# An encoder layer with expert retrieval on one core: Gelu of a score block emitted one block later, transposes of the picks later, gather share 0.68

## The chip, the cores and the metric

The kernel runs on one core of one Trainium2 chip. Its time is the device time of one launch in microseconds; the kernel before has a median of 1366.46 us over three runs (1363.83 to 1366.56). Five engines work side by side, each through its own queue in order: PE multiplies matrices, DVE and ACT work on elements, POOL issues the gathers and does small element work, SP issues the loads of weights and tables. An instruction at the head of a queue that waits for a semaphore holds back all that stand behind it.

## The reference

Two sequences (prompt and sample, 256 tokens each, width 1024) go through the same layer: a gated convolution and an attention with 16 meta tokens, both projected out and added to the input, and then an expert retrieval, which is where this case plays:

```
s = einsum('thpc,hpnc->thpn', q, subkeys)          # 8 heads, 2 halves, 128 keys each
sv, si = top_k(s, 16)                              # of each half
cv, cp = top_k(sv[0][:,None] + sv[1][None], 16)    # 16 pairs of a head: 128 experts a token
eidx  = si[0]*128 + si[1]  of these pairs;  gates = softmax(cv)
a   = gelu(einsum('thkd,td->thk', u_tab[eidx], x), approximate=False) * gates
out = einsum('thk,thkd->td', a, v_tab[eidx])
```

There are 16384 experts (128 times 128), each with a row of 1024 in `u_tab` and in `v_tab`.

## The kernel before, in words

The two sequences are computed in two ways. For the prompt's 256 tokens the picked rows are **gathered**: one gather fetches, for one pick k of a tile of 128 tokens, each token's row of u and v side by side (128 x 2048 f32, 1.05 MB, line 157). DVE multiplies the u half with the token and sums it (the dot, `grow<-grow,xg`), ACT takes Gelu and multiplies the gate (two instructions on `dots`), and DVE adds v times that weight to the token's accumulator (the value, `hg<-grow,dots,hg`). Two tiles times 128 picks make 256 such gathers. Four buffers hold them (`GBUF`), so gather n+4 is issued once value n has been added. When value 128 is done, the accumulator of tile 0 is written out (line 166, `out_yp<-hg`) and that of tile 1 is loaded into the same buffer (line 168, `hg<-hdram`); value 129 waits for both.

The sample's 256 tokens are computed **dense**, over all experts, in two stages that PE runs:

- The *score stage* (lines 913 to 928) has 128 blocks. Block j loads 512 KB of u (line 918), multiplies it with the tokens (8 fp32 matmuls `pSj<-xr,u`; the profile lists each as two rows) into one of four PSUM buffers of the pool `psS`, and ACT takes Gelu of it. Block j+4 needs that buffer again.
- The *value stage* (lines 939 to 953) has 128 blocks, each with 512 KB of v and matmuls `acc<-v,Al` or `acc<-v,Ah` into four accumulators.

Beside the score blocks a generator, `gates_dense`, works off the dense gates: it decodes the sample's picks into `idx_i` and `idx_j` (`fin1`, DVE work), transposes them on PE (lines 864 to 867, `pi` and `pg`), and then in 32 steps for each of two tiles builds one-hot rows on DVE and ACT (`oi`, `oj`, `gh`, `gl`), multiplies them on PE into a 128 x 128 table of gates for four tokens (8 fp16 matmuls `pgm`, a *gate group* below), and puts that into `Al` or `Ah`. Where a block's Gelu stands already, the group is multiplied onto it (columns below `r_done`); where not, the block's Gelu is multiplied by the gates that stand (`n = tau[0]` tokens have theirs): ACT writes Gelu of those to `pSj` itself and DVE forms the product (`Al<-pSj,Al`).

The order of the work is set by credits and then by a scheduler. After each score block `bg(3.5)` gives the generator 3.5 times `SBS` and the gathers 3.5 times `SS`; a step of the generator costs what it yields, a step of the gathers costs `GU` = 2.65. A step of the gathers emits the weight of one pick, the dot of the next, and the issue of a further gather; that issue also waits for the matmuls of the block last emitted (`pe_mark`). The scheduler of the tile framework then orders each engine's instructions. The value stage spreads the gathers that are left evenly: `want = left * (j + 1) // (P - 2)`.

Of the kernel before, what the change touches and what calls it, by code (L numbers as in the profile page):

```python
# [12 lines left out]
AF = mybir.ActivationFunctionType  # L13
ALU = mybir.AluOpType
# [22 lines left out]
SF = 0.5  # L37
SB0 = 0.35
SR = 0.6
SS = 0.64  # L40
SMAX = 0.7
SBS = 0.42

# [2 lines left out]
def encoder_layer(ctx: ExitStack, tc: tile.TileContext, xp, xs_, meta, vec, w_in, w_out, wq,  # L46
# [22 lines left out]
    dve = Recorded(nc.vector, last)  # L69
    act = Recorded(nc.scalar, last_act)  # L70

    def sb(name, bufs, side="left"):
        return tc.tile_pool(name=name, bufs=bufs, side=side, reuse_waits="tile")
# [32 lines left out]
    def wtile(name):  # L106
        return wp.tile([P, D], F32, tag="w", name=name)
# [16 lines left out]
    def mm(out, st_, mv, chunks=range(NC), split=False):  # L124

        terms = ((0, 0), (0, 1), (1, 0)) if split else ((0, 0),)
        n = 0
        for c in chunks:
            for a, b in terms:
                i = pe.matmul(out, st_(c, a), mv(c, b), start=(n == 0), stop=(n == NC * len(terms) - 1))  # L130
                n += 1
        pe_mark[0] = i
        return i
# [80 lines left out]
    def run_tasks(limit=None):  # L214
        while tasks and (limit is None or credit["b"] >= 0):
            try:
                credit["b"] -= next(tasks[0])
            except StopIteration:
                tasks.pop(0)

    def bg(us):
        if tasks:
            credit["b"] += us * share["b"]
            run_tasks(1)
        credit["a"] += us * (share["a"] if tasks else min(share["a"] + share["b"], SMAX))
        more(0.0)

    def more(us):
        credit["a"] += us
        while credit["a"] >= GU:  # L230
            credit["a"] -= GU
            gather()
# [558 lines left out]
    def A(j):  # L791
        return Al[:, j] if j < JH else Ah[:, j - JH]
# [52 lines left out]
    r_done = [0]  # L845
    tau = [0]

    def gates_dense():

        for t in range(2):  # L850
            yield from fin1(t)
        q1x.close()
        topk_left[0] = -1
        ogx = ExitStack()
        og = ogx.enter_context(sb("og", 1, "right"))
        io = og.tile([P, P], F16, name="io")
        act.dma_start(io, iota16)
        ident16 = og.tile([P, P], F16, name="ident16")
        dve.tensor_copy(ident16, ident)
        iv = io.rearrange("p (a r) -> p a r", r=2)  # L860
        v4 = lambda x: x.rearrange("p t (a r) -> p t a r", r=2)
        for t in range(2):
            pi = psg.tile([P, 2, P], F16, tag="g", name="pi")
            pe.transpose(pi[:, 0, :], idx_i[:, t], ident16)
            pe.transpose(pi[:, 1, :], idx_j[:, t], ident16)
            pg = psg.tile([P, P], F32, tag="g", name="pg")
            pe.transpose(pg, gate_all[:, 2 + t], ident)
            glo = og.tile([P, P], F32, tag="glo", name="glo")
            g16 = og.tile([P, OC, P], F16, tag="gl", name="g16", bufs=2)[:, 0, :]
            dup = og.tile([P, 3, P, 2], F16, tag="dup", name="dup")  # L870
            act.activation(g16, pg, AF.Copy, scale=GSH)
            dve.scalar_tensor_tensor(glo, pg, GSH, g16, op0=ALU.mult, op1=ALU.subtract)
            for r in range(2):
                act.activation(dup[:, 0:2, :, r], pi, AF.Copy)
                act.activation(dup[:, 2, :, r], g16, AF.Copy)
            yield 1.6
            for o in range(P // OC):
                s0 = o * OC
                oi = og.tile([P, OC, P], F16, tag="oi", name="oi", bufs=2)
                oj = og.tile([P, OC, P], F16, tag="oj", name="oj", bufs=2)  # L880
                gh = og.tile([P, OC, P], F16, tag="gh", name="gh", bufs=2)
                gl = og.tile([P, OC, P], F16, tag="gl", name="gl", bufs=2)
                sl4 = lambda k: dup[:, k, s0:s0 + OC, None, :].to_broadcast([P, OC, 64, 2])
                ib = iv[:, None, :, :].to_broadcast([P, OC, 64, 2])
                dve.tensor_tensor(v4(oi), sl4(0), ib, op=ALU.is_equal)
                dve.tensor_tensor(v4(oj), sl4(1), ib, op=ALU.is_equal)
                dve.tensor_tensor(v4(gh), v4(oj), sl4(2), op=ALU.mult)
                for q in range(OC):
                    act.activation(gl[:, q, :], oj[:, q, :], AF.Copy, scale=glo[:, s0 + q:s0 + q + 1])
                for q in range(OC // 4):  # L890
                    pg = psg.tile([P, 4, P], F32, tag="g", name="pgm")
                    for r in range(4):
                        k = 4 * q + r
                        pe.matmul(pg[:, r, :], oi[:, k, :], gh[:, k, :], start=True, stop=False)  # L894
                        pe.matmul(pg[:, r, :], oi[:, k, :], gl[:, k, :], start=False, stop=True)
                    a = t * P + s0 + 4 * q
                    n = r_done[0]
                    pj = pg.rearrange("p t j -> p j t")
                    for part, lo, hi in ((Al, 0, JH), (Ah, JH, P)):
                        m = min(max(n, lo), hi)  # L900
                        if m > lo:
                            av = part[:, 0:m - lo, a:a + 4]
                            dve.scalar_tensor_tensor(av, pj[:, lo:m], 1.0 / GSH, av, op0=ALU.mult, op1=ALU.mult)
                        if m < hi:
                            act.activation(part[:, m - lo:hi - lo, a:a + 4], pj[:, m:hi], AF.Copy, scale=1.0 / GSH)
                tau[0] = t * P + s0 + OC
                yield 1.3 + (4 * r_done[0] + 60) / 700
        ogx.close()

    tasks.append(gates_dense())  # L910
    share.update(a=SS, b=SBS)
    ut = {}
    for j in range(P):
        if j == 80:
            while topk_left[0] >= 0:
                next(tasks[0], None) is None and tasks.pop(0)
        ub = wtile("u")
        nc.sync.dma_start(ub, u_t[:, j])
        p = psS.tile([P, 256], F32, tag="S", name="pSj")
        mm(p, lambda c, k: ub[:, c * P:(c + 1) * P], xr1)  # L920
        n = tau[0]
        if n:
            act.activation(p[:, :n], p[:, :n], AF.Gelu)
            dve.tensor_tensor(A(j)[:, :n], p[:, :n], A(j)[:, :n], op=ALU.mult)
        if n < 256:
            act.activation(A(j)[:, n:], p[:, n:], AF.Gelu)
        r_done[0] = j + 1
        bg(3.5)
    run_tasks()

    vp = ctx.enter_context(sb("vp", 2, "right"))
# [97 lines left out]
```

## Time and profile before

| what | us or as named |
|---|---|
| median of three runs | 1366.46 |
| time of the profiled execution | 1362.99 |
| its span, first to last instruction | 1360.9 |
| busy PE, DVE, ACT, POOL | 1298.1, 1031.9, 437.4, 414.0 |
| first matmul of the score stage | 401.23 |
| first matmul of the value stage | 907.5 |
| end of the last matmul | 1357.1 |
| mean DMA rate over the span | 338 GB/s |

A row of a group of instructions reads: line, engine, operation, tile written and tiles read, count, busy time and mean duration, and the idle time of the engine just before with what ended it. A row of the timeline reads: start, duration, engine, line, operation, tiles, shapes, count, and in brackets the idle time before it. Line 63 is a helper through which all DVE and ACT instructions go, so these are told apart by their tiles. The ends of matmuls are modelled; their starts, and the distance between starts, are measured.

### The profile page before, as it was taken

What the parts mean: (1) busy time and instruction counts of PE and PEld (TensorE: products, weight loads), DVE (VectorE), ACT (ScalarE), POOL (GpSimd) and SP (SyncE); (2) the same over time, 40 slices, a digit from 0 to 9 for tenths busy, and PEclk for the clock granted to TensorE, in tenths of its full rate; (3) what the DMA queues carried; (4) which work ended last, traced back from release to release, by engine and by line L of the source; (5) the groups of instructions that cost most, each with busy time, mean ns of one, the idle gap of its engine ahead of it and who ended that gap; (6) DMA issues with size and microseconds to landing.
All of it is one profiled execution on the core that took longest, in us unless ns stands there. A gap on an engine that the chain in (4) does not pass through costs nothing. (4 is left out here: it accounts for less than half of the span.)

```text
span 1360.9 us, 17663 instructions
## 1 busy us (share of the span) xinstructions
PE 1298.1 (95%) x5870; PEld 927.9 (68%) x5870; DVE 1031.9 (76%) x2356; ACT 437.4 (32%) x1467; POOL 414.0 (30%) x480
## 2 busy tenths in 40 slices
PE   5999998998999887999999999999999999999998
PEld 5888986677888666888888888774443344444443
DVE  5656999776999889988888996676666665666665
ACT  4555533732221312555555543111111111111111
POOL 2111224331344342222221221223455523433331
PEclk9999999999999998999999999999999999999999
DMA  6434637577998999999999999999999999999997
GB/s 218 126 109 153 206 107 263 199 272 301 366 341 332 390 399 374 348 368 367 355 368 359 366 375 376 377 416 416 417 417 417 418 416 417 416 417 416 416 417 294
DMA packets 90234, 460.19 MB, mean 338 GB/s; under 512 B 10512, under 2 KB 11024, under 8 KB 57120
## 3 DMA queue, kind: packets, MB, share of 16 engines
q0 software_dynamic: 37296, 270.02, 49.7%
q1 hardware_dynamic: 50832, 182.33, 36.1%
q10 hardware_dynamic: 2016, 6.72, 1.3%
q8 instruction: 46, 0.75, 0.2%
q14 instruction: 44, 0.36, 0.1%
HBM read 454.81 MB, written 4.19 MB: 337 GB/s over the span
## 5 line engine op out<-in xcount | busy, mean ns | idle before, releaser
L157 POOL DMA_INDIRECT grow<-in_uv,eidx x256 | 331.9, 1297 | 694.8 <-PE acc L947 118.1
L130 PE MATMUL pSj<-xr,u 128*128 128x256 f32 x2048 | 465.6, 385 | 12.6 <-ACT Al L63 10.5
L130 PEld LDWEIGHTS pSj<-xr,u 128*128 128x128 f32 x2048 | 386.3, 192 | 68.7 <-ACT Al L63 14.5
L63 DVE SCALAR_TENSOR_TENSOR grow<-grow,xg 128x1024 f32<-128x1024 f32 x256 | 312.5, 1221 | 143.6 <-DMA grow<-in_uv,eidx 138.6
L63 DVE SCALAR_TENSOR_TENSOR hg<-grow,dots,hg 128x1024 f32<-128x1024 f32 x256 | 327.9, 1281 | 77.4 <-ACT dots L63 67.9
L947 PE MATMUL acc<-v,Al 128*128 128x512 f32 x752 | 329.9, 596 | 1.8
L947 PEld LDWEIGHTS acc<-v,Al 128*128 128x128 f32 x752 | 140.6, 190 | 190.6 <-issue 164.2
L63 ACT ACTIVATE dots<-dots 128x1 f32<-128x1 f32 x256 | 51.6, 202 | 552.2 <-DVE grow L63 551.2
L947 PE MATMUL acc<-v,Ah 128*128 128x512 f32 x272 | 118.0, 594 | 0.2
L947 PEld LDWEIGHTS acc<-v,Ah 128*128 128x128 f32 x272 | 51.3, 190 | 66.7 <-issue 62.1
L63 ACT ACTIVATE gl<-oj,glo 128x128 f16<-128x128 f16 x256 | 88.8, 393 | 10.9 <-DVE oj L63 5.1
L63 ACT ACTIVATE dots<-dots,gate_all 128x1 f32<-128x1 f32 x256 | 75.1, 294 | 7.5 <-ACT dots L63 0.6
L63 DVE TENSOR_TENSOR wlo<-w,whi 128x1024 fp32r<-128x1024 f32 x42 | 51.0, 1217 | 19.9 <-ACT whi L63 13.9
L63 ACT ACTIVATE pSj<-pSj 128x256 f32<-128x256 f32 (+39 forms) x94 | 26.6, 284 | 110.7 <-PE pSj L130 110.7
L130 PE MATMUL pqq<-xr,w 128*128 128x256 f32 x256 | 59.5, 385 | 0.7 <-DMA w<-in_wq 0.7
L130 PEld LDWEIGHTS pqq<-xr,w 128*128 128x128 f32 x256 | 48.2, 194 | 7.3 <-DMA w<-in_wq 1.1
L63 ACT ACTIVATE whi<-w 128x1024 fp32r<-128x1024 f32 x42 | 43.9, 1055 | 20.5 <-PE pqq L130 9.5
L130 PE MATMUL pc<-xT,w 128*128 128x258 f32 (+1 forms) x192 | 47.5, 390 | 1.1 <-DVE rb L63 0.6
L130 PEld LDWEIGHTS pc<-xT,w 128*128 128x128 f32 x192 | 34.9, 192 | 8.6 <-issue 2.5
L130 PE MATMUL pqq<-xr,whi 128*128 128x256 f32 x128 | 37.2, 292 | 0.0
L130 PE MATMUL pqq<-xrl,whi 128*128 128x256 f32 x128 | 36.4, 285 | 0.3 <-DVE xrl L63 0.3
L894 PE MATMUL pgm<-gh,oi 128*128 128x128 f16 x256 | 35.5, 219 | 1.3 <-DVE gh L63 1.3
(268 smaller groups left out, 1539.3 us busy)
## 6 DMA issues: line engine op xcount, KB each, us to landing
u<-in_u_t SPq DMA_DIRECT2D x128, 512.0 KB, 6.8
v<-in_v_n SPq DMA_DIRECT2D x128, 512.0 KB, 14.9
w<-in_w_in SPq DMA_DIRECT2D x36, 512.0 KB, 4.3
w<-in_wq SPq DMA_DIRECT2D x32, 512.0 KB, 5.0
w<-in_w_out SPq DMA_DIRECT2D x16, 512.0 KB, 4.8
grow<-in_uv,eidx POOLq DMA_INDIRECT x256, 9.2
hdram<-h ACTq DMA_DIRECT2D x3, 512.0 KB, 3.0
h<-in_xp SPq DMA_DIRECT2D x2, 512.0 KB, 7.3
```

Source lines behind the costliest of these rows:

```text
L63: i = f(*a, **k)
L130: i = pe.matmul(out, st_(c, a), mv(c, b), start=(n == 0), stop=(n == NC * len(terms) - 1))
L157: i = pool.indirect_dma_start(out=r, out_offset=None, in_=uv, in_offset=bass.IndirectOffsetOnAxis(ap=eidx[:, t, k:k + 1], axis=0))
L894: pe.matmul(pg[:, r, :], oi[:, k, :], gh[:, k, :], start=True, stop=False)
L947: i = pe.matmul(acc[t][q], A(j)[:, t * P:(t + 1) * P], vb[:, q * 512:(q + 1) * 512], start=j == 0, stop=j == P - 1, skip_group_check=True)
```

## The change

Three edits, all in the score stage. `SS` goes from 0.64 to 0.68. `gates_dense` yields 4.0 once after the decode, ahead of everything that leads to the transposes. And the Gelu of block j, with its product, is emitted after the matmuls of block j+1 (function `experts`); `r_done` counts accordingly.

```diff
-SS = 0.64
+SS = 0.68
...
         q1x.close()
         topk_left[0] = -1
+        yield 4.0
         ogx = ExitStack()
...
-    ut = {}
+    late = []
+
+    def experts(j, p):
+
+        n = tau[0]
+        if n:
+            act.activation(p[:, :n], p[:, :n], AF.Gelu)
+            dve.tensor_tensor(A(j)[:, :n], p[:, :n], A(j)[:, :n], op=ALU.mult)
+        if n < 256:
+            act.activation(A(j)[:, n:], p[:, n:], AF.Gelu)
+        r_done[0] = j + 1
+
...
         mm(p, lambda c, k: ub[:, c * P:(c + 1) * P], xr1)
-        n = tau[0]
-        if n:
-            act.activation(p[:, :n], p[:, :n], AF.Gelu)
-            dve.tensor_tensor(A(j)[:, :n], p[:, :n], A(j)[:, :n], op=ALU.mult)
-        if n < 256:
-            act.activation(A(j)[:, n:], p[:, n:], AF.Gelu)
-        r_done[0] = j + 1
+        late.append((j, p))
+        if len(late) > 1:
+            experts(*late.pop(0))
         bg(3.5)
+    experts(*late.pop(0))
     run_tasks()
```

What the scheduler makes of it is seen in three places. First, on PE, the first transposes (`pi`, `pg`) and the first gate group. Before:

```order
L130 MATMUL pSj<-xr,u 128x256 x256
L864 LDWEIGHTS idx_i
L864 MATMUL pi<-ident_4995,idx_i 128x128
L865 LDWEIGHTS idx_j
L865 MATMUL pi<-ident_4995,idx_j 128x128
L867 MATMUL pg<-ident,gate_all 128x128
L130 MATMUL pSj<-xr,u 128x256 x16
L894 LDWEIGHTS oi
```

And with the change:

```order
L130 MATMUL pSj<-xr,u 128x256 x280
L865 LDWEIGHTS idx_i
L865 MATMUL pi<-ident_5054,idx_i 128x128
L866 LDWEIGHTS idx_j
L866 MATMUL pi<-ident_5054,idx_j 128x128
L868 MATMUL pg<-ident,gate_all 128x128
L130 MATMUL pSj<-xr,u 128x256 x10
L895 LDWEIGHTS oi
```

At 8 matmuls a block the transposes stand behind block 35 instead of 32 blocks, and the first gate group behind 36.25 blocks instead of 34.

Second, on DVE, from the last row of the decode (`idx_j<-Ah`) to `gh` of the first gate group. Before:

```order
L63 TENSOR_TENSOR idx_j<-Ah 128x128
L63 SCALAR_TENSOR_TENSOR grow,dots<-grow,xg_1560 128x1024
L63 SCALAR_TENSOR_TENSOR hg_1564<-grow,dots,hg_1564 128x1024
L63 SCALAR_TENSOR_TENSOR glo<-pg,g_5003 128x128
L63 SCALAR_TENSOR_TENSOR grow,dots<-grow,xg_1560 128x1024
L63 TENSOR_TENSOR oi<-dup,io 128x512
L63 TENSOR_TENSOR oj<-dup,io 128x512
L63 TENSOR_TENSOR oi<-dup,io 128x512
L63 TENSOR_TENSOR gh<-oj,dup 128x512
```

With the change, from the row behind `idx_j`:

```order
L63 SCALAR_TENSOR_TENSOR grow,dots<-grow,xg_1560 128x1024 x2
L63 SCALAR_TENSOR_TENSOR hg_1564<-grow,dots,hg_1564 128x1024 x2
L63 SCALAR_TENSOR_TENSOR grow,dots<-grow,xg_1560 128x1024
L63 SCALAR_TENSOR_TENSOR hg_1564<-grow,dots,hg_1564 128x1024
L63 SCALAR_TENSOR_TENSOR grow,dots<-grow,xg_1560 128x1024
L63 SCALAR_TENSOR_TENSOR glo<-pg,g_5062 128x128
L63 SCALAR_TENSOR_TENSOR grow,dots<-grow,xg_1560 128x1024
L63 SCALAR_TENSOR_TENSOR hg_1564<-grow,dots,hg_1564 128x1024
L63 TENSOR_TENSOR oi<-dup,io 128x512
L63 TENSOR_TENSOR oj<-dup,io 128x512
L63 TENSOR_TENSOR oi<-dup,io 128x512
L63 TENSOR_TENSOR gh<-oj,dup 128x512
```

Where two dots and one value stood ahead of the first `gh`, five dots (65 to 69) and four values (65 to 68) stand now.

Third, on DVE, the switch of the accumulator from tile 0 to tile 1; the tile's first value (number 129) is the first row that writes the new `hg`. Before, from that row on:

```order
L63 SCALAR_TENSOR_TENSOR hg_7901<-grow,dots,hg_7901 128x1024
L63 SCALAR_TENSOR_TENSOR Al<-pgm,Al 128x94x4
L63 SCALAR_TENSOR_TENSOR Ah<-pgm,Ah 128x17x4
L63 SCALAR_TENSOR_TENSOR grow,dots<-grow,xg_7854 128x1024
L63 SCALAR_TENSOR_TENSOR hg_7901<-grow,dots,hg_7901 128x1024
L63 TENSOR_TENSOR Ah<-pSj,Ah 128x256
L63 SCALAR_TENSOR_TENSOR grow,dots<-grow,xg_7854 128x1024
L63 SCALAR_TENSOR_TENSOR hg_7901<-grow,dots,hg_7901 128x1024
L63 TENSOR_TENSOR Ah<-pSj,Ah 128x256
```

With the change, from value 130 on:

```order
L63 SCALAR_TENSOR_TENSOR hg_7652<-grow,dots,hg_7652 128x1024
L63 SCALAR_TENSOR_TENSOR Ah<-pgm,Ah 128x10x4
L63 SCALAR_TENSOR_TENSOR grow,dots<-grow,xg_7605 128x1024
L63 SCALAR_TENSOR_TENSOR hg_7652<-grow,dots,hg_7652 128x1024
L63 TENSOR_TENSOR Ah<-pSj,Ah 128x228
L63 SCALAR_TENSOR_TENSOR Al<-pgm,Al 128x94x4
L63 SCALAR_TENSOR_TENSOR Ah<-pgm,Ah 128x11x4
L63 SCALAR_TENSOR_TENSOR grow,dots<-grow,xg_7605 128x1024
L63 SCALAR_TENSOR_TENSOR hg_7652<-grow,dots,hg_7652 128x1024
L63 TENSOR_TENSOR Ah<-pSj,Ah 128x232 x2
L63 TENSOR_TENSOR oi<-dup,io 128x512
L63 TENSOR_TENSOR gh<-oj,dup 128x512
```

Before, the new accumulator's first values have nothing of the gates behind them but the putting away of the last group. With the change, the one-hot work of gate group 59 (the last row, `gh`) stands behind values 129 to 132 and dot 133, and on PE that group stands behind 108 blocks. Further on, 156 gathers are issued by the end of the score stage's last block where it was 150. ACT's order of Gelus and weights is the same as before up to the Gelu of block 24; from block 25 on each Gelu stands behind one more weight.

## The prediction

> **What bounds the kernel now.** I read the chain of waits first, then the busy times by stretch, then PE's waits in the score stage.
>
> ```profile
> span 1360.9 us, 17663 instructions
> ```
> ```profile
> 907.50 103.01 PE acc L947 x240
> 1010.51 0.02 issue
> 1010.53 18.50 DMA v<-in_v_n
> ...
> 1329.36 27.75 PE acc L947 x64
> 1357.11 0.02 issue
> ```
>
> The chain ends on the value stage. 30 of its blocks (8 rows each) take 103.01 us, 3.434 each; 128 would take 439.5. The stage runs from 907.5 to 1357.1, 449.6 us: 10.1 us are lost there, and where they are lost the chain leaves PE for loads of v. The stretches show why:
>
> ```profile
> 401.00:537.00 136.00, 117.33 (x520) 99.53 (x519) 122.83 (x322) 30.84 (x106) 49.70 (x56) 0.96 0.97 381
> 549.00:845.00 296.00, 294.72 (x1722) 257.04 (x1721) 256.31 (x524) 155.54 (x638) 66.90 (x66) 1.00 0.95 364
> ```
> ```profile
> 957.00:1007.00 50.00, 50.00 (x118) 22.14 (x117) 32.72 (x39) 6.47 (x26) 24.10 (x13) 1.00 1.02 417
> 1007.00:1057.00 50.00, 49.17 (x109) 19.36 (x108) 33.47 (x40) 6.47 (x26) 25.78 (x14) 1.00 1.02 417
> ```
>
> The columns are the busy time of PE, PEld, DVE, ACT, POOL, then the clock, the DMA share and GB/s. In the value stage the DMA stands at 417 GB/s. A block needs 0.524 MB of v, and 109 dots are left for 126 blocks (106 gathers not yet issued by the order, three under way), 0.865 x 1.049 MB: 1.431 MB in 3.434 us is 417 GB/s. So PE and DMA are level there, and PE gives way for 10 us. In the score stage it is 364 to 381 GB/s: a gather moved there finds room. PE is full from 549 to 845 and DVE 87% busy. Only ahead of 549, beside the decode, PE has holes:
>
> ```profile
> PE pSj L130 <- ACT Al L63: 10.5, 6, 4.2
> PE pi L864 <- DVE ident L63: 8.0, 1, 8.0
> PE pSj L130 <- DVE Ah L63: 2.0, 4, 0.9
> ```
> ```profile
> 401.23 41.69 PE L130 MATMUL pSj<-xr,u 128*128 128x256 f32 x192
> 447.09 22.67 PE L130 MATMUL pSj<-xr,u 128*128 128x256 f32 x96 [4.17 <-ACT Al L63]
> ...
> 505.73 22.67 PE L130 MATMUL pSj<-xr,u 128*128 128x256 f32 x96 [3.46 <-ACT Al L63]
> 536.44 0.27 PE L864 MATMUL pi<-ident,idx_i 128*128 128x128 f16 x1 [8.04 <-DVE ident L63]
> ...
> 536.82 8.83 PE L130 MATMUL pSj<-xr,u 128*128 128x256 f32 x32
> ```
>
> Twelve blocks in 41.69 us are 3.47 each. The two blocks behind the 8.04 us hole take 8.83 instead of 6.94: a long hole costs 1.9 us more behind it.
>
> **Gelu one block later.** The holes that it could close are the waits on ACT, up to block 26 (505.73). The block that waits needs the Gelu of four blocks back, so the last of them needs Gelu 22. ACT's order is the same up to Gelu 24: nothing changes there, 0 us. From Gelu 25 each stands behind one more weight, so behind one more dot of DVE. Blocks 29 to 34 find theirs just in time: blocks there come every 3.47 us, dots every 3.5 to 4. I take 0; at worst it delays PE where it waits longer anyway (next part).
>
> **First transposes and first gate group.** PE waited 8.04 us for the `ident` cast on DVE. Now three more blocks (10.4 us) stand ahead, the cast some 5 us later behind two more values and a dot: this wait shrinks to about 3 us. But the first gate group now stands only 1.25 blocks behind the transposes, and on DVE behind five dots and four values in place of two and one. These gathers go through four buffers, so they form a chain:
>
> ```profile
> 524.21 0.97 POOL L157 DMA_INDIRECT grow<-in_uv,eidx  x1 [2.34 <-DVE Ah L63]
> ...
> 536.41 1.12 POOL L157 DMA_INDIRECT grow<-in_uv,eidx  x1 [2.76 <-DVE ident L63]
> ```
> ```profile
> 533.22 1.22 DVE L63 SCALAR_TENSOR_TENSOR grow<-grow,xg 128x1024 f32<-128x1024 f32 x1 [0.38 <-DMA grow<-in_uv,eidx]
> 534.37 1.28 DVE L63 SCALAR_TENSOR_TENSOR hg<-grow,dots,hg 128x1024 f32<-128x1024 f32 x1
> ```
> ```profile
> DMA to landing us min/median/max: 5.9/9.2/13.5
> ```
>
> Dot 63 starts at 533.22 as its gather, issued at 524.21, lands (9.0 us); value 62 ends at 535.65, in both orders, and frees the buffer of gather 66, issued 0.76 later at 536.41. It lands at 545.4; dot 66 (1.22) and value 65 (1.28) end at 547.9; gather 69 is issued at 548.7 and lands 5.9 to 9.0 us later; dot 69, value 68 and the four one-hot rows (under 0.42 each) end at 558.5 to 561.7. I take 559.5, since PE then stands and loads no u. PE reaches the group at about 548. From 559.5: half a us for the group, 2.6 for the rest of block 36, 1.9 for the hole, half a us for the next group: block 37 at 565.
>
> ```profile
> 557.80 3.67 PE L130 MATMUL pSj<-xr,u 128*128 128x256 f32 x16
> 561.76 3.67 PE L130 MATMUL pSj<-xr,u 128*128 128x256 f32 x16
> ```
>
> Before, block 37 starts at 557.80, with four groups done (a block with a group takes 3.96, so a group 0.49); with two it were 556.8. Cost: **+8 us**, 6 to 10.
>
> **The switch of the accumulator.** With 0.68, a block under the gates carries 3.5 x 0.68 / 2.65 = 0.898 gathers in place of 0.845: 6 more over 112 blocks. So value 128 falls into the gate groups, near block 103 instead of 109.
>
> ```profile
> 835.81 1.28 DVE L63 SCALAR_TENSOR_TENSOR hg<-grow,dots,hg 128x1024 f32<-128x1024 f32 x1
> ...
> 855.62 1.28 DVE L63 SCALAR_TENSOR_TENSOR hg<-grow,dots,hg 128x1024 f32<-128x1024 f32 x1 [9.27 <-DMA hg<-hdram]
> ```
> ```profile
> 837.39 0.57 POOL L166 DMA_DIRECT2D out_yp<-hg  x1 [1.91 <-DVE hg L63]
> ...
> 848.60 0.57 POOL L168 DMA_DIRECT2D hg<-hdram  x1 [9.35 <-DMA out_yp<-hg]
> 857.66 1.80 POOL L157 DMA_INDIRECT grow<-in_uv,eidx  x1 [8.50 <-DVE Ah L63]
> ```
> ```profile
> 864.91 1.22 DVE L63 SCALAR_TENSOR_TENSOR grow<-grow,xg 128x1024 f32<-128x1024 f32 x1 [2.07 <-DMA grow<-in_uv,eidx]
> ```
>
> Value 128 ends at 837.09 and value 129 starts 18.5 us later: tile 0 is written, tile 1 read back, one after the other. DVE's queue stands. Before, little was behind it: all gate groups but the last two had their `gh`, the others got theirs in time, and PE lost 0.9 us on `Ah` and the small rest of the 2.0 us above. With the change, `gh` of group 59 stands behind value 129, values 130 to 132 and dot 133, whose gather needs value 129's buffer. From the end of value 128: 18.5 + 1.28 + 0.76 to its issue, 7.25 to landing (857.66 to 864.91), then 1.22 + 1.28 and four short rows (1.7): 32 us. PE meanwhile: value 128 ended 3.2 us behind the start of the block that follows the newest group then put away (833.89, below); that is now group 55, behind 102 blocks. Up to group 59 PE has 6 blocks and three groups less these 3.2: 20.8 + 1.5 - 3.2 = 19.1 us.
>
> ```profile
> 833.89 7.12 PE L130 MATMUL pSj<-xr,u 128*128 128x256 f32 x32
> ```
>
> PE stands 12.9 us and loses 1.9 more; the 2.0 us on `Ah` fall away. Cost: **+12.5 us**. The bounds: with both transfers as quick as the quickest 512 KB of the trace (3.0 and 4.3 us to landing), the hold is 8 us, PE's stand 2.4 and the cost 0.5; with a gather at 13.5 us it is 19. The row of the same transfers decides for the middle.
>
> ```profile
> hdram<-h ACTq DMA_DIRECT2D x3, 512.0 KB, 3.0
> w<-in_w_in SPq DMA_DIRECT2D x36, 512.0 KB, 4.3
> ```
>
> The Trainium skill, DMA: Bandwidth & Descriptors, "Anatomy of one DMA", puts a DMA from this path at some 2 us and its bytes over 436 GB/s. By it the two transfers would take an estimated 6.4 us together, the hold 7, and the sum below would be about 12 us smaller. The rows, 11.2 and 7.0 us beside a full DMA, speak against it here.
>
> **Second transposes, steady groups.** 1.38 blocks lie between transposes and group before and now, and DVE's rows ahead are alike (one dot, one value): 0. Six more gathers are 15 us of DVE in 296, 87% becomes 92%: 0 under PE's 100%.
>
> **Value stage.** Now 103 dots are left: 0.817 x 1.049 + 0.524 = 1.381 MB a block, 402 GB/s at PE's pace, below 417. Of 10.1 us lost I give back **9** (6 to 10.1).
>
> **Sum.** +8 + 12.5 - 9 = +11.5 us. On the profiled execution's 1362.99 (2.1 beside its span) that is 1374.5; the median of the runs is 3.5 above that execution, which would make 1378. I say **1376**. What a measurement of this kernel can tell from no change is about 0.2%, 2.7 us.
>
> **Rivals.**
> *The switch finds cover*, with transfers that land in 3 to 4 us each: the sum loses 12, to -0.5: 1362.5 to 1366. For it: 3.0 and 4.3 us for equal sizes elsewhere; against it: the rows of the same two transfers, 11.2 and 7.0 us. 15%. The Trainium skill's rule on a DMA's fixed cost, cited above, would bring it about.
> *Faster: DVE has the one-hot rows ready.* If the five gathers ahead of `gh` had landed early, the first group would not wait, the 8.04 + 1.9 us would be gone, and with a covered switch the value stage's 9 come on top: 1363 - 19 = 1344. It decides if the first group runs before 550. DVE's 122.8 busy of 136 us there, and the buffer chain, speak against it. 11%.
> *The value stage gives nothing back*, as v loads queue behind gathers all the same (18.5 us to landing in the chain): +20.5, 1384 to 1387. The level of 417 against 402 speaks against it. 12%.
> *The Gelu edit does nothing* holds in my forecast already for blocks up to 24.
>
> **How the numbers follow.** The forecast (1369 to 1383 by its own bounds) gets 62%, the rivals 15, 11 and 12. The range 1358 to 1386 leaves out the faster rival and the top. Slower: forecast and third rival, 74%, plus the upper end of the first, 1: 75%. Same: 11%, from the first rival. Faster: the second and the low end of the first, 14%.
>
> **What would show it.** PE's waits: one hole of 9 to 13 us before the first `pgm`, ended by `gh`; one of 8 to 17 before group 59, with DVE's value 129 waiting for `hg<-hdram`; the holes of 447 and 505 unchanged; value stage at 440 to 443 us with hardly a wait for v and under 417 GB/s. Wrong it is if PE runs through blocks 36 or 108, or if the waits up to block 26 shrink.

## The result, and the profile after

The changed kernel takes 1386.26 us (median of four runs, 1383.63 to 1387.3), the kernel before beside it 1366.51 (1363.83 to 1370.03): a ratio of 1.0137, 95% interval 1.0111 to 1.0162, or about 20 us more. The profiled execution of the changed kernel took 1387.3, its span is 1385.3, which is 24.4 more than the span before.

Of these 24.4 us, 4.3 lie ahead of anything that was changed: the first matmul of the score stage starts at 405.56, before at 401.23. The program up to there is the same. In the fourteen executions profiled in this study that start lies between 401.2 and 410.8, so it is a difference between executions; that before is the earliest of all. What remains for the change is 20.1, which agrees with the medians. Below, both kernels are counted from that first matmul.

PE's waits between 401 and 960 us, changed kernel (wait, what ended it: us in all, times, longest):

```profile
PE pgm L895 <- DVE gh L63: 25.9, 4, 11.8
PE pSj L130 <- ACT Al L63: 11.7, 6, 5.0
PE pSj L130 <- DMA u<-in_u_t: 5.2, 1, 5.2
PE pi L865 <- DVE ident L63: 2.5, 1, 2.5
PE pgm L895 <- DVE oi L63: 0.8, 1, 0.8
```

The six waits on ACT up to block 26 are as before (11.7 and 10.5). The 8.0 us at the first transposes have shrunk to 2.5, and 25.9 us stand now ahead of gate groups. Where, the timeline of PE tells (start, duration, work, and in brackets the idle time before it):

```profile
545.77 0.22 PE L865 MATMUL pi<-ident,idx_i 128*128 128x128 f16 x1 [2.49 <-DVE ident L63]
...
551.13 1.13 PE L130 MATMUL pSj<-xr,u 128*128 128x256 f32 x4 [1.50 <-ACT Al L63]
563.94 0.27 PE L895 MATMUL pgm<-gh,oi 128*128 128x128 f16 x1 [11.68 <-DVE gh L63]
```
```profile
839.64 0.23 PE L895 MATMUL pgm<-gh,oi 128*128 128x128 f16 x1 [0.76 <-DVE oi L63]
859.04 0.27 PE L895 MATMUL pgm<-gh,oi 128*128 128x128 f16 x1 [11.82 <-DVE gh L63]
```
```profile
904.96 20.38 PE L130 MATMUL pSj<-xr,u 128*128 128x256 f32 x83 [5.24 <-DMA u<-in_u_t]
```

One hole of 11.7 us before the first gate group, one of 11.8 before group 59, and one of 5.2 at block 118 that waits for a load of u. The third of the four waits in the first line, 2.09 us, stands at the second transposes; the fourth is 0.3 us. The chain of waits passes through the last two holes and then through the value stage without a gap:

```profile
839.96 5.49 DMA hg<-hdram
...
845.55 1.28 DVE hg L63
...
847.60 7.65 DMA grow<-in_uv,eidx
...
858.66 0.35 DVE gh L63
...
889.39 15.44 DMA u<-in_u_t
...
941.96 439.48 PE acc L956 x1024
```

Behind the long holes PE runs slower for a while. The stretches of the switch (busy PE, PEld, DVE, ACT, POOL, then the granted clock, DMA share, GB/s):

```profile
840.00:850.00 10.00, 7.22 (x37) 6.05 (x34) 4.45 (x7) 2.25 (x10) 2.62 (x3) 1.00 0.72 257
850.00:860.00 10.00, 0.95 (x9) 1.06 (x10) 6.53 (x15) 2.46 (x11) 2.50 (x3) 0.57 0.82 317
860.00:870.00 10.00, 10.00 (x43) 8.23 (x43) 7.68 (x16) 4.04 (x16) 0.94 (x1) 0.74 0.71 242
```

The clock is 0.74 in the ten microseconds behind the hole, and the two blocks there took 16.24 and 6.56 us, from start to start, where 3.96 each is usual: 14.9 us lost, 11.8 by the hole and 3.1 by the clock.

By equal work done, the change costs and saves:

| place | predicted us | measured us |
|---|---|---|
| holes up to block 26 | 0 | -0.2 |
| first transposes and first group | +8 | +8.6 |
| steady groups | 0 | 0 |
| second transposes | 0 | +1.4 |
| switch: the hole, 0.8 at `oi`, slower clock behind | +12.9 + 1.9 | +15.8 |
| end of the score stage | -2.0 | +4.4 |
| value stage | -9 | -10.1 |
| sum | +11.5 | +19.9 |

The prediction had rounded the hole, the clock and the -2.0 to +12.5. For the end of the score stage, blocks 118 and 119 took 8.86 and 5.76 us in place of 3.45: 7.7 lost, against 3.3 lost before between blocks 114 and 122.

### The profile page after: what moved, and what is told of

The parts are those of the page before. It is cut to its first block, busy times and chain, and to the rows that moved or that the text cites. A ratio compares the mean times of both kernels' runs of the same rounds, so it can differ in the third digit from the quotient of the medians.

```text
span 1385.3 us, 17684 instructions
## 1 busy us (share of the span) xinstructions
PE 1299.4 (94%) x5870; PEld 938.1 (68%) x5870; DVE 1028.3 (74%) x2357; ACT 435.1 (31%) x1467; POOL 379.1 (27%) x480
## 5 line engine op out<-in xcount | busy, mean ns | idle before, releaser
L157 POOL DMA_INDIRECT grow<-in_uv,eidx x256 | 297.1, 1160 | 748.6 <-PE acc L956 235.1
L130 PE MATMUL pSj<-xr,u 128*128 128x256 f32 x2048 | 469.9, 387 | 17.2 <-ACT Al L63 11.7
L956 PE MATMUL acc<-v,Al 128*128 128x512 f32 x752 | 322.9, 592 | 0.0
L63 DVE TENSOR_TENSOR wlo<-w,whi 128x1024 fp32r<-128x1024 f32 x42 | 51.1, 1218 | 19.9 <-ACT whi L63 13.9
L895 PE MATMUL pgm<-gh,oi 128*128 128x128 f16 x256 | 36.3, 222 | 26.6 <-DVE gh L63 25.9
L63 ACT ACTIVATE Al<-pSj 128x256 f32<-128x256 f32 (+29 forms) x94 | 30.0, 323 | 57.8 <-DVE Al L63 57.2
L895 PEld LDWEIGHTS <-oi 128*128 128x128 f16 x256 | 25.3, 99 | 28.8 <-DVE oi L63 24.1
```

The source lines that it names most:

```text
L63: i = f(*a, **k)
L157: i = pool.indirect_dma_start(out=r, out_offset=None, in_=uv, in_offset=bass.IndirectOffsetOnAxis(ap=eidx[:, t, k:k + 1], axis=0))
L956: i = pe.matmul(acc[t][q], A(j)[:, t * P:(t + 1) * P], vb[:, q * 512:(q + 1) * 512], start=j == 0, stop=j == P - 1, skip_group_check=True)
```

## The experiments

Each ratio is to the kernel before, run beside it on the same chip, with its 95% interval. All traces are of one execution each. First each of the three edits alone, and the whole change without the switch.

**The share alone.**

```diff
-SS = 0.64
+SS = 0.68
```

> Only the gather share goes to 0.68; Gelu and transposes stay where they were. Theory (order on DVE): the cost sits where DVE rows of the gathers stand ahead of one-hot rows. Here three dots and two values lie between the decode and the first gh, and the first gate group comes 2.1 blocks behind the transposes: PE's wait for the ident cast grows from 8 to about 12 us, no wait before the group, +5. At the switch of the accumulator gh of groups 60 and 61 is ahead of value 129, gh of group 62 behind values 129 to 131: a hole of about 6 us and 2 behind it, +7. The value stage falls to 440, -10. Sum about +3 us over the kernel before (0 to +7), so about 1369. Rival (load): more gathers beside the gates cost by themselves, as DVE or the DMAs are too full; then this run shows most of the change's +20 us, with losses spread over the blocks.

1371.12 us against 1367.01; ratio 1.0037, 1.0009 to 1.0064. Value stage nearly without waits (439.7 us from its first to its last matmul, before 449.2), and yet 4 us slower: the score stage takes it all. That is not most of the change's 20 us, and the score blocks between the holes run at their usual pace, so the rival (load) falls. PE's longest wait there, and the one at the switch:

```profile
PE pi L864 <- DVE ident L63: 13.5, 1, 13.5
PE pSj L130 <- ACT Al L63: 8.5, 6, 3.4
PE pSj L130 <- DMA u<-in_u_t: 4.3, 1, 4.3
PE pgm L894 <- DVE gh L63: 3.7, 2, 2.4
```

The first transposes wait 13.5 us, not 8.0. On DVE the `ident` cast, on which they wait, stands behind 64 dots and 64 values instead of 63 and 62, and it starts 5.0 us later after the first matmul than before. At the switch the hole is 2.4 us where about 6 had been expected, and a load of u is late here too.

**The later transposes alone.**

```diff
         topk_left[0] = -1
+        yield 4.0
```

> Only the extra yield ahead of the transposes; share 0.64, Gelu as before. Theory: the 8 us wait for the ident cast goes, but the first gate group at 36.25 blocks waits about 8 us for gh behind four dots, +1 together; the gate groups end at block 115 instead of 111, so that the switch of the accumulator comes with groups 63 and 64 still to do: a hole of about 10 us at block 113 and 2 to 3 behind it; the value stage stays at 450. Sum +8 to +15 us. Rival (load): the share is as before, so no cost, and the gain of the transposes' wait shows: -5 to -10 us.

1370.61 us; ratio 1.0028, 1.001 to 1.0046. Slower, so the rival falls, but by less than the theory's 8 us in the median. The profiled execution is the slowest of the ten (1380.82), so its holes can be longer than those of the median. In it the hole has gone from the transposes to the group, as expected:

```profile
562.08 0.27 PE L895 MATMUL pgm<-gh,oi 128*128 128x128 f16 x1 [10.73 <-DVE gh L63]
```

A second hole of 9.4 us stands before a group at 871.7; value 129 runs at 863.6 after 8.4 us of waiting for its load: three blocks' delay alone already brings the last groups behind the switch.

**The later Gelu alone** (function `experts` of the change, nothing else).

> Only Gelu and product one block later. Theory: ACT's order is unchanged up to the Gelu of block 24, so the holes at blocks 12 and 26 stay; the first gate group stays at block 34, about 2 us later by the cast; all gh are ahead of value 128, so the switch costs what it did; the value stage stays at 450. Sum 0 to +3 us. Rival (what the edit could do): PE's waits for a score buffer vanish, 10.5 us of waits and up to 4 us behind them, -8 to -14 us.

1371.85 us; ratio 1.004, 1.0015 to 1.0066. Not the 0 to 3 of the theory in the median, and not the rival's gain. The holes up to block 26 (11.5 us) did not shrink. The first transposes wait 10.6 us instead of 8.0; the cast stands behind one more value. The larger wait that is new stands at the switch, here for DVE and for PE:

```profile
865.49 1.28 DVE L63 SCALAR_TENSOR_TENSOR hg<-grow,dots,hg 128x1024 f32<-128x1024 f32 x1 [11.18 <-DMA hg<-hdram]
```
```profile
867.17 8.18 PE L130 MATMUL pSj<-xr,u 128*128 128x256 f32 x26 [5.79 <-DVE Ah L63]
```

All groups are done, but the product of a score block now stands on DVE behind value 129, and PE waits for that block's PSUM buffer.

**No switch.** The changed kernel neither writes tile 0 nor loads tile 1's start at the switch; both tiles are summed in one accumulator, which is written to both places at the end. So tile 0's result is not computed.

```diff
         if t == 0 and k == P - 1:
-            pool.dma_start(yp[0:P, :], gctx["h"])
-            h = gc.tile([P, D], F32, tag="hg", name="hg1")
-            pool.dma_start(h, hdram[0])
-            gctx["h"] = h
+            pass
...
+    nc.sync.dma_start(yp[0:P, :], gctx["h"])
     nc.sync.dma_start(yp[P:2 * P, :], gctx["h"])
```

> The changed kernel without the switch of the accumulator: tile 0's sum is not written out there and tile 1's start is not loaded, both tiles add into one accumulator, which is written twice at the end. Left out: one write and one load of 512 KB beside the score stage. Theory: the hole before gate group 59 (11.8 us and 3 behind it) goes, and with it the crowd of gathers that met the two early v loads, so that block 118 doesn't wait (5.2 and 2.3): 16 to 24 us below the changed kernel, 1363 to 1371. The hole of 11.7 us before the first group stays. Rival (load): PE waits in the same blocks for other reasons, at most 5 us below the changed kernel.

1369.5 us; ratio 1.0019, 0.9995 to 1.0042, against 1.0137 of the change: some 16 us are the switch. The 10.1 us before the first group stay, the hole of 11.8 is gone, and from the end of the score stage on it is the changed kernel: a wait of 4.3 us for u, and 439.0 us from the first to the last matmul of the value stage, as there. In this the expectation was wrong: u is late with no switch at all.

The three edits alone cost 0.37, 0.28 and 0.40%, together 1.05; the change costs 1.37. With these intervals it can't be told that the edits do worse together than one by one. Each brings the switch and PE's need for DVE closer together by itself, and each pays for it.

**Value 129 four gathers later.** At the switch, four gathers' worth of credit are taken off once.

```diff
             gctx["h"] = h
+            credit["a"] -= 4 * GU
```

> The changed kernel, and four gathers' worth of the pace taken away once when the accumulator is switched, so that value 129 stands behind the one-hot rows of group 61 on VectorE and no longer behind those of group 58; 152 gathers stand in the program by the end of the score stage and no longer 156. Theory (the hold is a matter of where value 129 stands): the hole of 11.8 us before group 59 and the 3 us of cold TensorE behind it and the 0.8 us at the switch fall away, the value stage gives 0 to 3 us back; 1369 to 1375 us, about what the kernel with no switch took (1369.5). Rival (VectorE is late there in any case, and the hold only shows it): the hole moves to group 61 or 62 and stays over 6 us; 1379 to 1387 us.

1373.53 us against 1362.6; ratio 1.007, 1.005 to 1.0091. The hole before group 59 is gone and not replaced; all that is left of the waits on `gh` is essentially the first group's:

```profile
PE pgm L896 <- DVE gh L63: 15.9, 4, 12.5
PE pSj L130 <- ACT Al L63: 13.8, 9, 4.3
PE pSj L130 <- DMA u<-in_u_t: 3.4, 1, 3.4
```

So it is the place of value 129 in DVE's queue that costs, not the transfers as such: both are still made. By the ratios 9 us come back, where leaving out the switch gave 16. In this execution, the slowest of the five, some 7 us more than in the changed kernel's are lost ahead of block 104, where the order of PE's, DVE's and ACT's work is the same in both; from there on some 18 us less are lost.

**The two early loads of v held back** until the matmuls of block 119.

```diff
-        nc.sync.dma_start(vb, vn3[:, j])
+        i = nc.sync.dma_start(vb, vn3[:, j])
+        if j in (2, 5):
+            sync_dep(i, marks[119])
```

(`marks` holds the last matmul of each block.)

> The changed kernel, and the two loads of v that were issued between the loads of u 117 and u 118 wait for the matmuls of block 119, so that no load of u stands behind them. Theory (the loads of v that come early make the load of u late): the hole of 5.2 us at block 118 and the 2.3 us of cold TensorE behind it go, nothing is late in their place because the first blocks of the value stage come 30 us later; 1377 to 1381 us. Rival (the queues are full of gathers there, and some load of u is late whichever goes first, or the v loads are late next at the head of the value stage): 1383 to 1388 us, with a hole of 4 us or more elsewhere after 880 us.

1382.49 us; ratio 1.015, 1.0116 to 1.0183. The time lies between the two expectations, the ratio is no lower than that of the change, and the hole that the rival named is there. SP's queue in that stretch:

```profile
885.64 17.59 SPq L931 DMA_DIRECT2D u<-in_u_t  x6
903.34 0.84 SPq L951 DMA_DIRECT2D v<-in_v_n  x2
906.36 10.69 SPq L931 DMA_DIRECT2D u<-in_u_t  x4
```

Once more the u behind the two v is late: PE waits 4.5 us, now at block 124. It does not matter which u it is: whichever stands behind the two v finds 1.05 MB more asked of a DMA that was busy already. In the changed kernel:

```profile
890.00:895.00 5.00, 5.00 (x25) 4.41 (x24) 2.77 (x4) 0.77 (x3) 1.08 (x2) 1.00 1.02 424
...
900.00:905.00 5.00, 0.04 (x1) 0.07 (x1) 3.54 (x7) 0.62 (x3) 0.94 (x1) 0.77 1.03 422
```

Before, the two loads came at 845.5, in the pause of the gathers at the switch, and no u was late.

**Share and later transposes, Gelu in its own block.**

> The share 0.68 and the later transposes without the later Gelu and product. Value 129 stands behind the rows of group 58, as in the changed kernel (of the parts alone: behind 61 with the share, 62 with the transposes, 64 with the Gelu). Theory (share and transposes each bring the switch nearer to the groups, and only together ahead of groups 59 to 61): a hole of 8 to 13 us before group 59, 1379 to 1387 us, far more than the parts' own +4 and +4. Rival (each part costs what it cost alone and the Gelu has its share in the hole): 1372 to 1376 us, with a hole under 5 us at the switch.

1378.52 us; ratio 1.0115, 1.0097 to 1.0133. The time is near the theory's, the hole is not: in the profiled execution, the quickest of this kernel (1371.61, its span 1369.5), PE waits 2.64 us at group 59, which is under the rival's 5 us. The hole in the slower executions was not profiled. DVE's rows say why:

```profile
840.83 1.29 DVE L63 SCALAR_TENSOR_TENSOR hg<-grow,dots,hg 128x1024 f32<-128x1024 f32 x1 [0.89 <-DMA hg<-hdram]
842.03 0.42 DVE L63 TENSOR_TENSOR oi<-dup,io 128x512 f16<-128x512 f16 x1
842.36 1.28 DVE L63 SCALAR_TENSOR_TENSOR hg<-grow,dots,hg 128x1024 f32<-128x1024 f32 x1
...
843.86 1.28 DVE L63 SCALAR_TENSOR_TENSOR hg<-grow,dots,hg 128x1024 f32<-128x1024 f32 x1
...
845.63 0.42 DVE L63 TENSOR_TENSOR gh<-oj,dup 128x512 f16<-128x512 f16 x1
...
849.67 1.23 DVE L63 SCALAR_TENSOR_TENSOR grow<-grow,xg 128x1024 f32<-128x1024 f32 x1 [1.77 <-DMA grow<-in_uv,eidx]
```

The `gh` of group 59 stands behind values 129 to 131 (in the change behind 129 to 132), but ahead of the first dot whose gather had to wait for their buffers. That dot starts at 849.67; in the changed kernel the same `gh` stands behind it. So my expectation, which counted only the groups ahead of value 129, took half of the mechanism: the other half is the refill of the four gather buffers behind the hold. Here the write and the load also took only 4.1 and 4.7 us to landing, where they took 9.5 and 5.5 in the changed kernel.

**The share in two steps:** 0.56 up to the decode, 0.74 beside the gates, five gathers' worth off at the switch, v held, transposes and Gelu as before.

```diff
-    share.update(a=SS, b=SBS)
+    share.update(a=0.56, b=SBS)
...
         topk_left[0] = -1
+        share["a"] = 0.74
...
             gctx["h"] = h
+            credit["a"] -= 5 * GU
```

> The kernel before with another pace: share 0.56 until the picks are decoded, 0.74 from then on beside the gates, five gathers' worth taken away once at the switch of the accumulator, and the two early loads of v held to block 119; Gelu and transposes where they were. Five dots fewer stand ahead of the first group (62 against 67). Theory (the one-hot rows of the first group are late because VectorE waits its turn behind gathers at a full DMA rate, and the later gathers find room beside the gates): the hole before the first transposes shrinks from 8 to 13 us to 0 to 4 us, none at the switch, value stage 440 to 445 us; 1346 to 1358 us. Rival (VectorE is as full as the queues beside the gates, so a share of 0.74 makes the groups late): steady blocks over 3.96 us, 1362 to 1372 us.

1375.61 us; ratio 1.0107, 1.0076 to 1.0138. Slower than either expected. The transposes wait only 0.6 us, but the first group 14.1; and the groups further on are late too (PE 15.64 us busy of 20 from 800 to 820, before 20.00):

```profile
526.01 0.22 PE L867 MATMUL pi<-ident,idx_i 128*128 128x128 f16 x1 [0.60 <-DVE ident L63]
547.40 0.26 PE L897 MATMUL pgm<-gh,oi 128*128 128x128 f16 x1 [14.09 <-DVE gh L63]
```
```profile
530.57 1.23 DVE L63 SCALAR_TENSOR_TENSOR grow<-grow,xg 128x1024 f32<-128x1024 f32 x1 [3.69 <-DMA grow<-in_uv,eidx]
540.83 1.23 DVE L63 SCALAR_TENSOR_TENSOR grow<-grow,xg 128x1024 f32<-128x1024 f32 x1 [3.89 <-DMA grow<-in_uv,eidx]
```

Fewer gathers up to the decode do not help here: four dots still stand between the cast and the first `gh`, and those shown wait for their gathers. This run changes four things at once, so it does not show by itself that these dots make the group late. The next experiment takes them away.

**A pause ahead of the picks.** The changed kernel, and four gathers' worth of credit taken off once when the decode ends.

```diff
         topk_left[0] = -1
+        credit["a"] -= 4 * GU
         yield 4.0
```

> The changed kernel, and four gathers' worth of the pace taken away once when the second decode ends, ahead of the first transposes. Between the end of the decode and the rows of the first group one dot is left on VectorE (five dots and their values stand there now), and the switch comes later too: value 129 stands behind the rows of group 62. Theory (the first group waits for dots whose gathers have not landed, one after the other, not for a full VectorE): the hole of 11.7 us before the first group shrinks to 2 to 6 us; the hole before group 59 goes as with value 129 four gathers later; 152 gathers by the end of the score stage; 1357 to 1367 us. Rival (the hole is what it takes to copy, transpose and build the rows, wherever the dots stand): hole still 8 us or more, 1369 to 1376 us.

1366.09 us against 1367.89; ratio 0.9996, 0.997 to 1.0021, 1.4% below the change. The hole of 11.7 us before the first group is not smaller but gone:

```profile
545.65 0.22 PE L866 MATMUL pi<-ident,idx_i 128*128 128x128 f16 x1 [2.46 <-DVE ident L63]
...
549.33 0.22 PE L896 MATMUL pgm<-gh,oi 128*128 128x128 f16 x1
```

From transposes to group it takes 3.7 us, not 18.2. One dot stands between the decode and the first `gh`, in place of five. So the rival, that building the rows takes that long, falls. The switch came later, but not late enough: 8.45 us before group 63, which stands behind value 129 and a refilled dot.

```profile
850.36 1.28 DVE L63 SCALAR_TENSOR_TENSOR hg<-grow,dots,hg 128x1024 f32<-128x1024 f32 x1 [5.17 <-DMA hg<-hdram]
858.56 1.22 DVE L63 SCALAR_TENSOR_TENSOR grow<-grow,xg 128x1024 f32<-128x1024 f32 x1 [1.84 <-DMA grow<-in_uv,eidx]
```

**Share and pause without the rest of the change.**

```diff
-SS = 0.64
+SS = 0.68
...
         topk_left[0] = -1
+        credit["a"] -= 4 * GU
```

> The kernel before with the share 0.68 and the same pause of four gathers' worth ahead of the first transposes; transposes and Gelu where they were. Value 129 stands behind the rows of group 64, as in the kernel before, and 152 gathers stand in the program by the end of the score stage, not 150. Theory (the share gives the value stage back its 9 us, and the pause takes away what the share cost at the first group and at the switch): hole before the first transposes 8 to 13 us as with the share alone, none of it added before the first group, no hole at the switch, 1357 to 1365 us, the kernel before 1363 to 1367. Rival (the pause only moves the stall: the first group waits as long once the transposes are done): 1368 to 1374 us.

1367.13 us; ratio 1.0014, 0.9982 to 1.0047, no different from the kernel before within the interval, and above the 1357 to 1365 us expected. No hole at the switch, as expected, but 13.8 us at the first transposes, and the value stage is back at 446.0 us (148 gathers begun by then, 154 in the change).

**Two pauses.** The changed kernel with the pause of four at the picks and one of two at the switch.

```diff
             gctx["h"] = h
+            credit["a"] -= 2 * GU
...
         topk_left[0] = -1
+        credit["a"] -= 4 * GU
         yield 4.0
```

> The changed kernel with the pause of four gathers' worth ahead of the first transposes, and another of two at the switch of the accumulator. Rows of groups 61 to 63 stand ahead of value 129 and those of group 64 ahead of the first dot whose gather is issued behind value 129 (rows of 63 stand behind such a dot with the first pause alone). Theory (the hole of 8.5 us that the first pause left at group 63 is the refill of the gather buffers behind the hold): that hole and some 2 us of cold TensorE go, 150 gathers by the end of the score stage give 2 to 5 us back in the value stage; ratio to the kernel before 0.992 to 0.998, some 1356 to 1363 us. Rival (a hole of the same size comes at group 64, or the value stage gives it all back): 0.999 to 1.003.

1356.51 us against 1367.67; ratio 0.9924, 0.9909 to 0.994. That is faster than both kernels. All of PE's waits from 401 to 960:

```profile
PE pSj L130 <- ACT Al L63: 7.9, 4, 3.8
PE pSj L130 <- DVE grow L63: 5.5, 1, 5.5
PE pi L867 <- DVE ident L63: 0.8, 1, 0.8
PE pgm L897 <- DVE gh L63: 0.6, 2, 0.3
```

The gate groups wait 0.6 us in all. The value stage gives some back (443.1 us, against 439.0 in the change), and the wait at block 118 is still there: it is the line of 5.5 us. The line names a dot of DVE, but the load of u of that block, issued at 854.39, landed 15.7 us later, 0.1 us before PE went on at 870.21.

**Two pauses, Gelu back in its own block.**

> The same two pauses with the share 0.68 and the later transposes, and Gelu and product of a block back in the block itself. Theory (the later Gelu neither helps nor hurts but through the order in which the rows then stand): within 3 us of the kernel with two pauses, if no hole comes at the switch. Rival (the later Gelu costs by itself, as its own ratio of 1.004 suggests): 4 us or more below the kernel with two pauses.

1359.17 us; ratio 0.9936, 0.992 to 0.9953. The intervals of the two overlap: whether the later Gelu is worth anything by itself is not settled, but it does not cost the 4 us that it cost alone.

## Why the prediction was right, and where it was off

The forecast was slower, and it is slower, but by 20 us where 9.5 had been stated: 1376 was named, 1386.26 came, a quarter of a microsecond above the top of the range. The two large holes and the gain of the value stage came close to what had been worked out; one term had the wrong sign.

**First transposes and first group** (predicted +8, measured +8.6). The chain of gather buffers was the right mechanism, row by row: the transposes' wait fell to 2.5 us (predicted about 3), the group's `gh` ended at about 563.9 where 558.5 to 561.7 had been given, 4.3 us of it the later start of this execution. The pause at the picks shows the cause by taking it away.

**The switch** (predicted 12.9 for the hole, measured 11.8). From the end of value 128 the prediction had 18.5 us to value 129, 7.25 for the refill and 32 to `gh`. Measured are 15.7 (829.86 to 845.55), 7.65 and 29.2, and PE came to group 59 after 17.4 us where 19.1 were worked out. That the hole came out within 1.1 us is in part luck: `gh` was 2.8 us earlier than worked out, and PE 1.7. Both halves, the hold and the refill, are confirmed: by moving value 129 behind three more groups, and by the run in which the refilled dot stands behind group 59 instead of ahead. Mis-sized was what lies behind the hole: 1.9 us, taken from a hole of 8.0 us, came to 3.1. The length of the hole does not explain it: behind the hole of 11.7 us before the first group it was 2.3.

**The step that failed** is "the 2.0 us on `Ah` fall away", as the last of the switch's cost. They did, but the term ended there. What the two v loads meet that SP issues early was not asked. Before, they fell into the pause of the gathers at the switch; now the switch is over by then, the gathers are back and catch up, and a load of u lands 15.44 us after its issue, behind v. That is +4.4 in place of -2.0, the largest part of the 8.4 us by which the sum fell short. Holding v back only moved the wait to the u that then stood behind the pair. The traces of all fourteen executions agree with this account. In the three in which the pair was issued before value 129 had started (before, the later Gelu alone, share and pause), PE did not wait for the u behind it. In the eleven in which it was issued after that, PE waited 0.9 to 5.6 us for the u right behind it, also in the run with no switch. The DMA moves 405 to 424 GB/s there in the changed kernel. That the pair meets the gathers is thus shown by comparing runs; no run moved the pair back into a pause and left the rest as it was.

**Second transposes** were taken as 0 and cost 1.4. Their wait of 2.09 us is again on `gh`.

**The value stage** (predicted -9, measured -10.1): PE runs through it without a wait. One sign that was named did not come: the rate is not under 417 GB/s at its start.

```profile
957.00:1007.00 50.00, 50.00 (x117) 22.07 (x117) 33.26 (x40) 6.46 (x26) 16.52 (x12) 1.00 1.02 417
```

At first the DMA still runs at that rate and gets ahead of PE: v lands 8.8 us after its issue in the median, before 14.9. The rate falls to 408 to 403 GB/s from 1042 us on, near the 402 that had been worked out.

**The Gelu edit** was taken as 0. The waits that it could close stayed, as argued; but alone it cost 0.40%, in its trace mostly through a product behind value 129, which the prediction did not look for. What it costs within the change is not settled: the two runs with two pauses, with and without it, do not differ beyond their intervals.

**The rivals.** *The switch finds cover* did not happen here: the write took 9.5 and the load 5.5 us. The Trainium skill, DMA: Bandwidth & Descriptors, "Anatomy of one DMA", gives an estimated 6.4 us for the two. The quickest pair seen, in the kernel with share and later transposes, took 8.7. *DVE has the one-hot rows ready* was the right lever with the wrong condition: the gathers need not land early, it is enough that no dot that waits for its gather stands ahead of `gh`. *The value stage gives nothing back* is refuted. Its time, 1384 to 1387, is the one that came, but by the end of the score stage and not by the value stage.

## What to carry to other kernels

An in-order queue that serves two streams is paced by whichever stands at its head: before a row that another engine is about to need, let no work stand that waits for a transfer of its own. Here taking four transfers' credit off once did that (ratio 0.9996 in place of 1.0137), and a lower share up to the picks, with other edits beside it, did not (1.0107). A hold on such a queue costs its own length and then the refill of the buffers that stood empty meanwhile; look for what is placed behind both. When a pause in one stream moves, ask which other loads lived in that pause.

## What was not expected of the hardware

The same write of 512 KB took 4.0 to 11.0 us to landing, and the load behind it 4.7 to 7.4, in the ten executions whose traces tell both, so a hold of this kind is not one number. Here it went with how busy the DMA was: the seven writes of 9.3 us and more fell where its share was 0.99 or more, the three of 4.0 to 4.4 us where it was 0.85 to 0.93.

What a hole costs PE beyond itself does not follow its length. Holes of 4.3 us and more behind block 26 cost 1.5 to 3.2 us more: the one of 14.1 us in the run with the share in two steps cost 1.9, and the one of 5.6 us in the same run 3.1. The granted clock was 0.69 to 0.85 in the ten microseconds behind ten of them. Of the holes of 2.1 to 2.7 us most left the blocks behind them at their usual pace, but not all. In the run with share and later transposes, one of 2.64 us cost nothing, with the clock at 1.00 behind it, and one of 2.16 us at block 113 cost about 1.8, with the clock at 0.83.
